# One stage of a hybrid encoder layer: channel sums by two fp32r products, finer pieces of the projections, and KT behind the weights' remainders

## The chip, the cores and the metric

One core of a Trainium2 chip runs the whole layer. The metric is the device time of one execution in microseconds. The kernel before took 826.56 us (median of 3 runs, 826.28 to 828.94).

The engines are named as in the profile: PE (matrix products; PEld is its loading of weights), DVE (vector), ACT (scalar, activations), POOL (GpSimd), SP (issues most DMAs).

## The reference, cut to what matters

One layer over 528 tokens (16 learned ones and 512 of the sequence) of width 1024. A projection of the normalised input feeds two branches of eight heads each, a delta-rule recurrence (RWKV-7) and attention with forgetting (FoX), and a gate for each channel and branch:

```python
u = rmsnorm(h, norm_mix);  proj = u @ w_in
# recurrence: per head and token
kk = k * k_k;  kk = kk / max(sqrt(sum(kk * kk, over the head's 64 channels)), 1e-12)
S = S * w + (S @ -kk) * (kk * a) + v * k;   y = S @ r
bonus = sum(r * k * r_k, over the head's 64 channels) * v
# attention: per head
q = q * rsqrt(mean(q * q, over the head's 64 channels) + eps) * q_gain;  k likewise
# both branches joined, then a squared-ReLU MLP
merged = sig(g_A) * (y_rw @ w_out_rw) + sig(g_B) * (y_fx @ w_out_fx)
h = h + merged @ w_o;  h = h + square(relu(rmsnorm(h) @ w_up)) @ w_down
```

The sums over a head's 64 channels in it (for `kk`, for the bonus, for q and for k) are what the change computes in another way.

## The kernel before, in words

Channels lie on the 128 partitions (two heads in each block of 128 channels, a "pair"), tokens along the free dimension. Most large products take their fp32 operands as two fp32r tensors, an upper part `hi` and a remainder `lo = x - hi`, and add three products (`passes`): hi by hi, hi by lo, lo by hi. ACT makes `whi` and DVE the remainder `wlo` of each piece of weights (`convert`, L548 and L549).

The program has three stages. The first makes the normalised input and the first two projections. The second, from about 30 to 401 us, is the one that the change edits. The third multiplies the two branches' outputs with their output weights (`po`, L1260), and then runs `w_o` and the MLP.

In the second stage several streams are written as generators: the recurrence of four pairs (`recurrent`: `decay`, `keys`, `rows`, `scores`, `bonus` for a pair, `inverse` for a group of two pairs), the sequential part of a group (`chain`) with its `group_norm`, the attention (`attention`), its normalised queries and keys (`fox_features`, `Fox.normed`), and the projections (`projections`), which hold 24 blocks of 128 output columns for the two branches and 16 for the gates. A block takes 24 products for a part of its tokens: branch blocks mostly in two parts of 264 tokens, gate blocks and queries in one of 512.

A stream yields where PE would have to wait, with a function that tells when its data are there by the planner's own clock (`Clock`, with a cost for each engine and the rings of buffers). `Turns.run` takes at each step the first stream by rank whose data are ready: the chain has rank 0, the recurrence 1, attention 2, the features 3, group norm and the splitting of y 4, the projections 8. So the products of the projections fill whatever the others leave, and the last of them are the gate blocks, which nobody needs before the third stage. PE's order in this stage is the planner's order (a manual schedule), and PE takes its instructions in that order: where one has to wait, all behind it wait. The other engines' order is set by priorities in the tile framework.

A projection stream yields before every second `k` in blocks of 264 columns, that is after six products, and before each `k`, after three, in blocks of 512 (L571 and L572 hold the condition and the yield).

The channel sums are products with `ones_blk`, a matrix of two 64x64 blocks of ones, in plain fp32: `pkk` (L906) of the squares of the recurrence's keys, two parts of 264 tokens a pair; `pssq` (L680) of the attention's queries (512 tokens) and keys (two parts of 264); `pbn` (L940) of the bonus, 512 tokens, with `ones_blk` scaled by `r_k` (`rkb`, L934).

`BK` and `KT` are the scaled keys of a pair; `scores` multiplies `BK` with the rows `L` (`psr`, L957) and transposes `KT` (`pbt`, L964). `KT` has one buffer, as have `lc` and `tha`.

The end of the stage: the chain's last step ends in `py` (L1136, L1087); ACT copies it to `y_rw`; `group_norm` (mean, variance, an inverse square root by Newton steps, all on DVE but one square) makes `ysq`; PE transposes it (`pyt`, L1161) and makes the output gate (`pg`, L1164); DVE multiplies, and `divided` splits the result into `ys`, which `po` reads.

## Time and profile before

| | |
|---|---|
| median of 3 runs | 826.56 us |
| the profiled execution | 826.42 us |
| its span, first to last instruction | 824.6 us |
| mean granted clock of PE | 0.998 |
| PE busy in the span | 808.5 us (98%) |
| DVE, ACT, POOL busy | 606.5, 452.7, 120.6 us |
| last projection product to the first of the third stage | about 401 us |

Matmuls are pipelined: the duration of one is longer than the distance to the next, so costs on PE are read from the distance of starts. A line such as L579 is that of a helper or loop for all blocks; tiles tell them apart. The waits that end on PE count; those of other engines count only where PE comes to wait for them.

### The profile page before, as it was taken

Reading aid. Unit: us, or ns where it says so; the run is one execution under the profiler, and the core shown is the slowest. Engines: PE = TensorE matmul, PEld = TensorE weight load, DVE = VectorE, ACT = ScalarE, POOL = GpSimd, SP = SyncE. Lnnn points to the kernel's source line nnn. Section 1 sums busy time; section 2 is a strip of 40 time slices with the busy share of each in tenths; the row PEclk is TensorE's granted clock in tenths of the full one; section 3 lists DMA queues with packets and bytes.
Section 4 is the critical chain, followed back from the end, with each engine's and each line's share of the span. In section 5 each row is a group of like instructions: output and inputs, shape, how many; then the busy total and the mean of one; then the engine's idle time right before and its main releaser. Section 6 shows DMA issues by size and latency. Waiting matters only on the chain.

```text
span 824.6 us, 15506 instructions
## 1 busy us (share of the span) xinstructions
PE 808.5 (98%) x5886; PEld 667.4 (81%) x5886; DVE 606.5 (74%) x1196; ACT 452.7 (55%) x941; POOL 120.6 (15%) x124
## 2 busy tenths in 40 slices
PE   8989999998999999999999999999999999999998
PEld 6979887876987787678888889888888888888886
DVE  6787985687879855875366655875698679867988
ACT  7757538756575457754456534664445434543452
POOL 1021100010011000000032003100740074017300
PEclk9999999999999999999999999999999999999999
DMA  7222221211211412223687405523642365337532
GB/s 232 82 71 71 77 92 48 87 40 65 79 52 52 129 41 66 77 78 116 224 287 227 156 0 154 176 80 113 219 149 82 115 208 159 81 115 228 146 99 76
DMA packets 51483, 95.88 MB, mean 116 GB/s; under 512 B 5832, under 2 KB 7240, under 8 KB 51408
## 3 DMA queue, kind: packets, MB, share of 16 engines
q1 hardware_dynamic: 47680, 86.37, 33.2%
q0 software_dynamic: 1280, 4.20, 1.7%
q10 hardware_dynamic: 2448, 4.33, 1.5%
q8 instruction: 46, 0.75, 0.4%
q14 instruction: 29, 0.24, 0.1%
HBM read 88.56 MB, written 6.31 MB: 115 GB/s over the span
## 4 chain that ended last, share of the span: by engine, by line
PE 86%; DVE 5%; ACT 5%; issue 2%; DMA 1%; SPq 0%; POOL 0%; DVEq 0%; ACTq 0%
PE pj L579 22%; PE po L1350 21%; PE po L1477 12%; PE po L1260 5%; PE pd L1477 5%; PE po L1322 3%; PE pj L394 1%; PE po L1291 1%; PE pd L1291 1%; PE psc L748 1%; PE py L802 1%; PE psr L957 1%; PE ppt L785 1%; PE pch L1108 1%; DVE wlo L549 1%
## 5 line engine op out<-in xcount | busy, mean ns | idle before, releaser
L579 PE MATMUL pj<-uhi,whi 128*128 128x264 f32 (+1 forms) x480 | 164.2, 342 | 0.0
L579 PE MATMUL pj<-uhi,wlo 128*128 128x264 f32 (+1 forms) x480 | 153.8, 320 | 2.5 <-DVE wlo L549 2.5
L579 PE MATMUL pj<-ulo,whi 128*128 128x264 f32 (+1 forms) x480 | 153.8, 320 | 0.0
L242 DVE TENSOR_TENSOR wlo<-wraw,whi 128x512 fp32r<-128x512 f32 x84 | 80.3, 966 | 35.5 <-ACT whi L242 35.5
L579 PEld LDWEIGHTS pj<-uhi,whi 128*128 128x128 f32 x480 | 90.7, 189 | 12.8 <-issue 4.4
L579 PEld LDWEIGHTS pj<-uhi,wlo 128*128 128x128 f32 x480 | 90.7, 189 | 9.5 <-DVE wlo L549 2.9
L579 PEld LDWEIGHTS pj<-ulo,whi 128*128 128x128 f32 x480 | 90.9, 189 | 6.7 <-issue 1.6
L1350 PE MATMUL po<-zlo,whi 128*128 128x512 f32 (+1 forms) x248 | 94.8, 382 | 0.0
L1350 PE MATMUL po<-zhi,wlo 128*128 128x512 f32 (+1 forms) x248 | 94.8, 382 | 0.0
L1350 PE MATMUL po<-zhi,whi 128*128 128x512 f32 (+1 forms) x248 | 94.8, 382 | 0.0
L242 ACT CAST whi<-wraw 128x512 fp32r<-128x512 f32 x84 | 51.4, 617 | 55.7 <-PE po L1350 25.6
L548 ACT CAST whi<-wraw 128x512 fp32r<-128x512 f32 x78 | 47.8, 617 | 42.3 <-PE pj L579 41.6
L549 DVE TENSOR_TENSOR wlo<-wraw,whi 128x512 fp32r<-128x512 f32 x78 | 52.7, 685 | 23.7 <-ACT whi L548 23.0
L276 ACT CAST whi<-t 128x512 fp32r<-128x512 f32 x64 | 39.9, 623 | 44.5 <-DVE wlo L276 27.3
L1477 PE MATMUL po<-wlo,fhi 128*128 128x512 f32 (+1 forms) x164 | 63.4, 387 | 0.1
L1399 POOL TENSOR_TENSOR t<-traw 128x512 f32<-128x512 f32 x24 | 38.2, 1608 | 171.6 <-DMA traw<-in_wdn 171.6
L1477 PE MATMUL po<-whi,flo 128*128 128x512 f32 (+1 forms) x164 | 62.9, 384 | 0.0
L1477 PE MATMUL po<-whi,fhi 128*128 128x512 f32 (+1 forms) x164 | 62.3, 384 | 0.0
L276 DVE TENSOR_TENSOR wlo<-t,whi 128x512 fp32r<-128x512 f32 x64 | 43.6, 690 | 24.2 <-ACT whi L276 24.0
L1366 ACT CAST fhi<-R 128x768 fp32r<-128x768 f32 (+1 forms) x32 | 30.2, 944 | 45.2 <-DVE R L1373 25.3
L1350 PEld LDWEIGHTS po<-zhi,wlo 128*128 128x128 f32 x248 | 46.6, 188 | 9.1
L1350 PEld LDWEIGHTS po<-zhi,whi 128*128 128x128 f32 x248 | 46.6, 188 | 9.0
(330 smaller groups left out, 1708.6 us busy)
## 6 DMA issues: line engine op xcount, KB each, us to landing
wraw<-in_win SPq DMA_DIRECT2D x84, 256.0 KB, 2.7
wraw<-in_wup SPq DMA_DIRECT2D x60, 256.0 KB, 3.1
wraw<-in_wdn SPq DMA_DIRECT2D x48, 256.0 KB, 2.7
traw<-in_wdn SPq DMA_DIRECT2D x48, 256.0 KB, 3.5
gd<-gt ACTq DMA_DIRECT2D x16, 256.0 KB, 2.2
wraw<-in_wout SPq DMA_DIRECT2D x16, 256.0 KB, 3.5
gl<-gd SPq DMA_DIRECT2D x16, 256.0 KB, 3.0
traw<-in_wdn POOLq DMA_DIRECT2D x16, 256.0 KB, 3.2
```

What stands on the lines that cost most here:

```text
L242: casts.append((A.copy(hi, raw), low.tensor_tensor(lo, raw, hi.bitcast(F32), ALU.subtract)))
L276: return A.copy(hi, x), V.tensor_tensor(lo, x, hi.bitcast(F32), ALU.subtract)
L548: after(A.copy(hi, raw), last["ACT"])
L549: after(V.tensor_tensor(lo, raw, hi.bitcast(F32), ALU.subtract), last["DVE"])
L579: mm(po, a, b[:, k, a0:a1], start=n == 0, stop=n == 23)
L1260: mm(po, a, ys[k][:, b, :], start=n == 0, stop=n == 11)
L1291: mm(pd[i], a[:, k, 128 * i:128 * i + 128], b, start=k == 0 and n == 0, stop=k == 7 and n == 2)
L1322: mm(po, a[:, k, 128 * i:128 * i + 128], b[:, k, :], start=n == 0, stop=n == 23)
L1350: mm(po[:, t0:t1], a, b[:, k, t0:t1], start=n == 0, stop=n == 23)
L1366: A.copy(fhi[:, j, a:b], R[:, a:b])
L1399: eng.tensor_tensor(t, sums[c, pair] if c in (T1, T2) else c, d, ALU.add)
L1477: mm(x[i][:, cols], a[:, k, left, 128 * rows:128 * rows + 128], c[:, cols], start=start and k == 0 and n == 0, stop=stop and k == n_pairs ...
```

## The change

Each channel sum becomes two fp32r products with `ones_r` (`summed`): the squares are split into `hi` (a copy on ACT) and `lo` (a subtraction on POOL; for the bonus, on DVE). For the bonus, `r_k` moves from the matrix into the split, and `rkb` is gone. The split parts need room: they take the buffers of `KT`, or for the attention those of `lc` and `tha`, and `held` with `hold` says who has them; the streams `decay`, `keys`, `bonus`, `inverse` and `normed` wait for them. `KT`'s last multiplication and half of `L` stand, for the first pair, behind the last remainder `wlo` issued by then. The transposes of `KT` are planned 1.0 us later than its product. Projection blocks of 264 columns yield after every three products, those of 512 also inside a triple. For pairs after the first, the attention's values are asked for after the queries are normalised.

In the program built from it PE gets 24 more instructions in this stage (48 for 24), POOL 20, ACT 16; DVE has four two-operand ones in place of four scalings, and one copy. The DMAs are the same.

```diff
--- before.py
+++ after.py
+    ones_r = cp.tile([128, 128], F32R, name="ones_r")
...
+    def summed(po, hi, lo):
+        mm(po, ones_r, hi, start=True, stop=False)
+        mm(po, ones_r, lo, start=False, stop=True)
...
+        V.tensor_copy(ones_r, ones_blk)
...
+        low = [None]
...
-                after(V.tensor_tensor(lo, raw, hi.bitcast(F32), ALU.subtract), last["DVE"])
+                low[0] = V.tensor_tensor(lo, raw, hi.bitcast(F32), ALU.subtract)
+                after(low[0], last["DVE"])
...
                         for k in range(KB):
-                            if k % 2 == 0 or a1 - a0 > 300:
+                            if True:
                                 yield lambda f=po is None: max(ck.ready(*w[k // 4]), block_bank()[0] if f else 0.0)
...
                             for a, b in passes(wk(w, k), U):
                                 mm(po, a, b[:, k, a0:a1], start=n == 0, stop=n == 23)
                                 n += 1
+                                if n % 3 == 2 and a1 - a0 > 300:
+                                    yield lambda: 0.0
...
+        held = [0, 0]
+
+        def hold(i):
+            yield lambda: math.inf if held[i] else 0.0
+            held[i] = 1
...
             def normed(self, d, parts, gcol):
                 yield d["in"]
                 f, sq = d["f"], d["sq"]
-                yield lambda: max(ck.ready(sq), banks(len(parts)))
+                c0 = parts[0][0]
+                yield lambda: math.inf if all(held) else 0.0
+                at = held[0]
+                held[at] = 1
+                if at:
+                    hl = rp.tile([128, 2, T], F32R, name="fhl", tag="KT")
+                    hi, lo = hl[:, 0, :], hl[:, 1, :]
+                else:
+                    hi, lo = (rp.tile([128, T], F32R, name="f" + tag, tag=tag) for tag in ("lc", "tha"))
+                d["s"] = A.copy(hi[:, c0:], sq[:, c0:])
+                for a0, a1 in parts:
+                    G.tensor_tensor(lo[:, a0:a1], sq[:, a0:a1], hi[:, a0:a1].bitcast(F32), ALU.subtract)
+                yield lambda: max(ck.ready(lo), banks(len(parts)))
                 pin = None
                 for a0, a1 in parts:
                     pq = psm("pssq")[:, :a1 - a0]
-                    mm(pq, ones_blk, sq[:, a0:a1], start=True, stop=True)
+                    summed(pq, hi[:, a0:a1], lo[:, a0:a1])
...
+                held[at] = 0
...
+                q = yield from x.normed(x.dq, SEQ, qg8)
+                x.q_done.done = True
                 if p > 0:
                     x.ask_values()
-                q = yield from x.normed(x.dq, SEQ, qg8)
-                x.q_done.done = True
...
             def decay(self):
                 p = self.p
+                yield from hold(0)
...
             def keys(self):
 
                 p = self.p
+                yield from hold(1)
...
+                hl = rp.tile([128, 2, T], F32R, name="hl", tag="KT")
+                hi, lo = hl[:, 0, :], hl[:, 1, :]
+                s_ = A.copy(hi, sq[:, :T])
+                for hc in parts:
+                    G.tensor_tensor(lo[:, hc], sq[:, hc], hi[:, hc].bitcast(F32), ALU.subtract)
+                yield lambda: max(ck.ready(hl), banks(2))
+                for hc in parts:
                     pq = psm("pkk")[:, :HT]
-                    mm(pq, ones_blk, sq[:, hc], start=True, stop=True)
+                    summed(pq, hi[:, hc], lo[:, hc])
...
-                V.tensor_tensor(KT, BK, self.P[:, :, 63:64].unsqueeze(2).to_broadcast([128, NCH, 2, 64]), ALU.mult)
+                s_ = V.tensor_tensor(KT, BK, self.P[:, :, 63:64].unsqueeze(2).to_broadcast([128, NCH, 2, 64]), ALU.mult)
+                if p == 0:
+                    after(s_, low[0])
+
+                held[0] = 0
...
-                V.tensor_tensor(l0[:, :, 64:128], r3, P, ALU.mult)
+                s_ = V.tensor_tensor(l0[:, :, 64:128], r3, P, ALU.mult)
+                if self.p == 0:
+                    after(s_, low[0])
...
-                self.rkb = rp.tile([128, 128], F32, name="rkb")
-                after(V.tensor_scalar(self.rkb, ones_blk, self.col(C_RK), None, ALU.mult), last["DVE"])
...
             def bonus(self):
+                yield from hold(1)
+                hl = rp.tile([128, 2, T], F32R, name="hl", tag="KT")
+                hi, lo = hl[:, 0, :S], hl[:, 1, :S]
+                A.activation(hi, self.sq[:, :S], AF.Copy, scale=self.col(C_RK))
+                V.scalar_tensor_tensor(lo, self.sq[:, :S], self.col(C_RK), hi.bitcast(F32), ALU.mult, ALU.subtract)
+                yield lambda: max(ck.ready(hl), banks(1))
                 bp = psm("pbn")
-                mm(bp, rkb, self.sq[:, :S], start=True, stop=True)
+                summed(bp, hi, lo)
+                held[1] = 0
...
             def scores(self):
-                    yield lambda: max(ck.ready(KT), banks(1))
+                    yield lambda: max(ck.ready(KT) + 1.0, banks(1))
...
+                held[1] = 0
...
         def inverse(g, Bms, late):
+            yield from hold(1)
...
+            held[1] = 0
```

Line numbers in the rows below are those of each kernel (after the change `pj` is L588, `po` L1309).

**PE at the end of the second stage.** `pyt` and `pg` are the group norm's transposes and the gate product, `pj` a projection, `ppt` and `ppm` transposes of the attention's weights, `psc` its scores. Before, from the last group norm on:

```order
L1161 MATMUL pyt<-cs,ysq 128x128 x4
L1164 MATMUL pg<-lhi,lw_4209 128x256
L1164 MATMUL pg<-llo,lw_4209 128x256
L1164 MATMUL pg<-lhi,lw_4210 128x256
L1164 MATMUL pg<-lhi,lw_4213 128x256
L1164 MATMUL pg<-llo,lw_4213 128x256
L1164 MATMUL pg<-lhi,lw_4214 128x256
L579 MATMUL pj<-uhi,whi 128x512
L579 MATMUL pj<-ulo,whi 128x512
L579 MATMUL pj<-uhi,wlo 128x512
```

and the last rows ahead of the third stage:

```order
L579 MATMUL pj<-uhi,whi 128x512
L579 MATMUL pj<-ulo,whi 128x512
L579 MATMUL pj<-uhi,wlo 128x512
L1260 MATMUL po<-ys,whi 128x512 x2
L1260 MATMUL po<-ys,wlo 128x512
L1260 MATMUL po<-ys,whi 128x512 x2
```

With the change, from the last gate products on, first to the group norm:

```order
L777 MATMUL psc<-ka,qa 128x272 x2
L777 MATMUL psc<-ka,qa 128x256 x2
L588 MATMUL pj<-uhi,wlo 128x512
L588 MATMUL pj<-uhi,whi 128x512
L588 MATMUL pj<-ulo,whi 128x512
L588 MATMUL pj<-uhi,wlo 128x512
L812 MATMUL ppt<-cs,pm_452 48x128
L814 MATMUL ppt<-cs,pe_5166 128x128 x3
L814 MATMUL ppt<-cs,pe_5174 128x128 x3
L1210 MATMUL pyt<-cs,ysq 128x128 x4
L1213 MATMUL pg<-lhi,lw_4509 128x256
L1213 MATMUL pg<-llo,lw_4509 128x256
```

and from its last gate product on:

```order
L1213 MATMUL pg<-lhi,lw_4514 128x256
L812 MATMUL ppm<-cs,pm_453 48x128
L814 MATMUL ppt<-cs,pe_5360 128x128 x4
L814 MATMUL ppt<-cs,pe_5369 128x128 x4
L828 MATMUL py<-pTm,vm 64x512 x2
L831 MATMUL py<-pT_4920,vt 64x512
L1309 MATMUL po<-ys,whi 128x512 x2
L831 MATMUL py<-pT_4921,vt 64x512
L831 MATMUL py<-pT_4920,vt 64x384
```

Before, 69 gate products stand ahead of the last `pyt` and 57 between `pg` and `po`; with the change the last six stand around `psc`, and after them come `ppt`, `pyt`, `pg`, the attention's last products and `po`, with no projection among them.

**DVE under the same end.** `st`, `rsgy` and `rsgw` are the group norm's, `psc`, `pe` and `pT` the attention's softmax. Before, from the mean to the variance:

```order
L1146 TENSOR_REDUCE st_5133<-y_rw 128x8
L1171 SCALAR_TENSOR_TENSOR yT<-yT,pr,bv 128x256
L276 TENSOR_TENSOR ys<-y_rw,ys 128x512
L1172 TENSOR_TENSOR y_rw<-yT,pg 128x256
L1147 TENSOR_SCALAR st_5133<-st_5133 128x8
L1148 TENSOR_TENSOR y_rw<-y_rw,st_5133 128x2x256
L276 TENSOR_TENSOR ys<-py,ys 128x512
L276 TENSOR_TENSOR ys<-y_fx,ys 128x512
L1152 TENSOR_REDUCE st_5139<-ysq 128x8
L1153 TENSOR_SCALAR st_5139<-st_5139 128x8
```

With the change, in the same place:

```order
L788 ISA pe_5360,nm<-psc,nF_4923 128x272
L788 ISA nm 128x1
L1197 TENSOR_TENSOR y_rw<-y_rw,st_5327 128x2x256
L786 TENSOR_TENSOR psc<-psc,cs 128x128
L788 ISA pe_5369,nm<-psc,nF_4925 128x272
L788 ISA nm 128x1
L788 ISA pe_5360,nm<-psc,nF_4923,nm 128x256
L788 ISA nm 128x1
L1201 TENSOR_REDUCE st_5333<-ysq 128x8
L786 TENSOR_TENSOR psc<-psc,cs 128x128
L1202 TENSOR_SCALAR st_5333<-st_5333 128x8
L817 COPY pT_4920<-ppt 128x3x128
```

The attention's reductions over the last queries now stand between the group norm's instructions; before, there were splits of y.

**DVE around the first pair's KT.** `wlo` is a remainder of weights, `orr` and `ov` are projections' results. Before:

```order
L919 SCALAR_TENSOR_TENSOR BK<-tha,KT 128x9x64
L310 SCALAR_TENSOR_TENSOR orr<-pj,pr_65,tm 128x264
L921 TENSOR_TENSOR KT<-BK,P 128x1152
L930 TENSOR_TENSOR L_662<-orr,P 128x9x64
L549 TENSOR_TENSOR wlo<-wraw,whi 128x512 x2
L306 MEMSET tm 128x1
L549 TENSOR_TENSOR wlo<-wraw,whi 128x512
```

With the change:

```order
L557 TENSOR_TENSOR wlo<-wraw,whi 128x512
L971 TENSOR_TENSOR L_670<-orr,P 128x9x64
L950 SCALAR_TENSOR_TENSOR okk<-okk,pr,sq 128x528
L311 MEMSET tm 128x1
L968 SCALAR_TENSOR_TENSOR L_670<-okk,P 128x9x63
L969 TENSOR_SCALAR L_670<-okk 128x9
L955 SCALAR_TENSOR_TENSOR KT<-okk,lc 128x9x64
L315 SCALAR_TENSOR_TENSOR ov<-pj,pr_66,tm 128x264
L956 SCALAR_TENSOR_TENSOR BK<-tha,KT 128x9x64
L557 TENSOR_TENSOR wlo<-wraw,whi 128x512
L958 TENSOR_TENSOR KT<-BK,P 128x1152
L315 SCALAR_TENSOR_TENSOR ov<-pj,pr_66,tm 128x264
```

KT's product (`KT<-BK,P`) and the half of L from `orr` stood ahead of two remainders; now each stands right behind one.

More of the change, by code (lines that the diff above doesn't have):

```diff
@@ L902, in keys @@
                 s_ = act(sq[:, :T], okr, AF.Square, scale=self.col(C_KK))
-                yield lambda: max(ck.ready(sq), banks(2))
-                for hc in (slice(0, HT), slice(HT, T)):
+                parts = (slice(0, HT), slice(HT, T))
+                hl = rp.tile([128, 2, T], F32R, name="hl", tag="KT")
[5 more added lines that the diff above has]
+                for hc in parts:
                     pq = psm("pkk")[:, :HT]
-                    mm(pq, ones_blk, sq[:, hc], start=True, stop=True)
+                    summed(pq, hi[:, hc], lo[:, hc])
                     V.tensor_scalar(sq[:, hc], pq, 1e-24, None, ALU.max)
```

3 lines of the change are left out of this document (removed).

## The prediction

> **What bounds the kernel now.** I read the page first, then the busy time by stretches, the waits of PE, the chain that ended last, and then the timeline of single engines where the change touches them. The page, with the span and the busy row:
>
> ```profile
> span 824.6 us, 15506 instructions
> PE 808.5 (98%) x5886; PEld 667.4 (81%) x5886; DVE 606.5 (74%) x1196; ACT 452.7 (55%) x941; POOL 120.6 (15%) x124
> ```
>
> By stretches (columns: microseconds, then busy time and count of PE, PEld, DVE, ACT, POOL, then the granted clock, the DMA share and GB/s):
>
> ```profile
> 36.00:371.00 335.00, 325.72 (x3575) 265.26 (x3574) 258.36 (x672) 210.82 (x530) 19.27 (x28) 0.99 0.23 71
> 371.00:401.00 30.00, 30.00 (x141) 24.94 (x138) 14.91 (x33) 13.41 (x25) 0.00 (x0) 1.00 0.39 126
> ```
>
> The whole change lies in the stage from 36 to 401 us, in which one planner weaves the recurrence, the attention and the projections (`pj`) into PE's order. PE is idle there for 335.00 - 325.72 = 9.3 us, and not at all from 371 to 401. So two things set the end of the stage: PE's own work, and whether a filler remains for every wait. The chain of waits shows how large the filler was at the end:
>
> ```profile
> 371.14 15.89 PE pj L579 x69
> 387.46 0.72 PE pg L1164 x6
> 388.18 12.92 PE pj L579 x57
> 401.10 43.81 PE po L1260 x192
> ```
>
> After the attention's last product at 371 come 126 products of gate columns, 28.8 us with no wait in them, and under them the last half of the group norm is finished. This is the row I lean on most: the recurrence ends about 30 us before the stage does, and PE alone bounds the end.
>
> **The change, part by part.**
>
> *The sums.* One fp32 product becomes two fp32r products. Price of each, from the timeline of PE:
>
> ```profile
> 38.33 0.28 PE L579 MATMUL pj<-uhi,wlo 128*128 128x264 f32 x1
> 38.45 1.05 PE L906 MATMUL pkk<-sq,cs 128*128 128x264 f32 x4
> 39.46 0.28 PE L579 MATMUL pj<-ulo,whi 128*128 128x264 f32 x1
> 39.58 0.28 PE L579 MATMUL pj<-uhi,wlo 128*128 128x264 f32 x1
> 65.39 1.02 PE L940 MATMUL pbn<-sq,rkb 128*128 128x512 f32 x2
> 66.25 1.02 PE L680 MATMUL pssq<-fsq,cs 128*128 128x512 f32 x2
> ```
>
> Starts count, not durations. An fp32r product of 264 columns takes 0.12 us (39.46 to 39.58). From 38.45 to 39.46 lie two fp32 sums and one such product, so a sum takes 0.445 us; after the change 0.24, a saving of 0.20. A sum of 512 columns takes 0.86 us (65.39 to 66.25); two fp32r products of 512 take 2 x 0.227 = 0.454 (43.81 us for 192 in the chain above), a saving of 0.41. The counts (the records show two for each sum):
>
> ```profile
> L680 PE MATMUL pssq<-fsq,cs 128*128 128x264 f32 (+1 forms) x24 | 8.4, 459 | 0.0
> L906 PE MATMUL pkk<-sq,cs 128*128 128x264 f32 x16 | 4.2, 386 | 0.0
> L940 PE MATMUL pbn<-sq,rkb 128*128 128x512 f32 x8 | 4.1, 593 | 0.0
> ```
>
> That is 8 + 8 sums of 264 columns and 4 + 4 of 512: 16 x 0.20 + 8 x 0.41 = **6.5 us less PE work**. Bounds: none of it if PE waits instead, 6.5 if all is streamed.
>
> *Finer pieces.* PE pays for each change of form:
>
> ```profile
> 152.77 0.28 PE L579 MATMUL pj<-uhi,wlo 128*128 128x264 f32 x1
> 152.98 0.45 PE L1130 MATMUL pch<-y_fx,bkT 128*64 128x64 f32 x8
> 153.60 0.39 PE L579 MATMUL pj<-uhi,whi 128*128 128x264 f32 x1
> 153.82 0.28 PE L579 MATMUL pj<-ulo,whi 128*128 128x264 f32 x1
> ```
>
> Leaving `pj` costs 0.21 - 0.12 = 0.09, coming back 0.22 - 0.12 = 0.10. In PE's order the `pj` products stand in 94 pieces before and 127 after; counting every neighbour's form, the changes of form in the stage go from 233 to 253, since the new sums have the form of `pj` itself. 20 x 0.1 = **2 us more**; bounds 0 and 33 x 0.2 = 6.6.
>
> *The waits in the middle.* The part on KT and the finer pieces touch these two, the longest of PE's waits:
>
> ```profile
> PE pj L579 <- DVE wlo L549: 2.5, 1, 2.5
> PE pbt L964 <- DVE KT L921: 2.1, 2, 1.3
> ```
>
> ```profile
> 48.09 1.35 DVE L921 TENSOR_TENSOR KT<-BK,P 128x1152 f32<-128x1152 f32 x1
> 49.36 1.82 DVE L930 TENSOR_TENSOR L<-orr,P 128x576 f32<-128x576 f32 x1
> ```
>
> In the first pair KT and half of L, 3.1 us of DVE, ran ahead of the remainders that PE's next block needed. Now a remainder stands ahead of each. What is late next is KT itself: PE reaches KT's transposes one row of scores and one gate product after the scores may start, while DVE still has a remainder and KT's 1.35 us to do, so some tenths of the 2.5 us come back. The other pairs still have KT on their path, but only planned a microsecond later: of 2.1 us I take off 1.5. Together **3.5 us less**; bounds 0 (the wait only moves) and 9.3 (all idle time goes).
>
> *New work on ACT and POOL.* Sixteen copies on ACT and 20 subtractions on POOL. PE does not wait long for them: in PE's order 5 us or more of other products stand between the block that feeds a sum and the sum. But POOL's subtraction reads two operands from SBUF, and this is what such a thing does to DVE here:
>
> ```profile
> 43.92 1.80 POOL L920 TENSOR_TENSOR BK<-sg,lc 128x576 f32<-128x576 f32 x1 [8.01 <-ACT lc L893]
> 44.35 1.40 DVE L928 TENSOR_SCALAR L<-okk 128x9 f32<-128x9 f32 x1
> L928 DVE TENSOR_SCALAR L<-okk x4: 164/717/1399, 44.4 to 248.9; 128x9 f32<-128x9 f32 x4
> ```
>
> Nine elements a partition take 0.16 us alone and 1.40 us when POOL is at work: DVE stands until POOL is through. No row has a POOL subtraction of 264 columns; between nothing and the 1.80 us of the 576-column one, I take 0.8 in proportion, and 1.6 for the four of 512 columns: 16 x 0.8 + 4 x 1.6 = 19 us. If half of that falls on a DVE instruction, DVE loses some 10 us in the stage, in which it is 258 of 335 us busy. Little of that reaches PE: I take **1 us more**, bounds 0 and 10. [...]
>
> *The end of the stage.* Here the order decides. The holds put off pairs and sums, every put-off moment was filled with gate products, and nothing of the 126 remains: after the last six gate products come scores, transposes, the group norm's transposes, and the next stage. So the work that was covered is now waited for. Its length, from the timeline of PE and DVE before:
>
> ```profile
> 367.38 0.45 PE L1087 MATMUL py<-y_fx,Bm 64*64 64x64 f32 x8
> 368.70 0.68 DVE L1146 TENSOR_REDUCE st<-y_rw 128x8 f32<-128x512 f32 x1
> 377.17 0.69 DVE L1156 TENSOR_TENSOR ysq<-y_rw,rsgy 128x512 f32<-128x512 f32 x1
> 386.87 0.60 PE L1161 MATMUL pyt<-cs,ysq 128*128 128x128 f32 x4
> 392.54 0.69 DVE L276 TENSOR_TENSOR ys<-y_rw,ys 128x512 fp32r<-128x512 f32 x1 [0.24 <-ACT ys L276]
> ```
>
> From the last product of the recurrence to the normalised rows: 377.86 - 367.38 = 10.5 us. DVE did 3.7 us of other work in it; after the change it does the attention's softmax of the last 128 queries in the same stretch (estimated from the first two rows below: four reductions, two copies, and scalings and masks like them, some 4 us, against about 2 that leave), so 12 us. (The last two rows, from the chain of waits, are PE's cover, used below.)
>
> ```profile
> 334.43 0.43 DVE L759 CUSTOM_DVE_ANT_0 pe<-psc,nF 128x272 f32<-128x272 f32 x1
> 356.72 1.02 DVE L788 COPY pT<-ppt 128x384 f32<-128x384 f32 x2 [0.25 <-PE ppt L785]
> 348.84 1.09 PE psc L748 x8
> 316.57 0.87 PE ppt L785 x8
> ```
>
> PE has as cover the rest of that product (0.3), six products (6 x 0.227 = 1.4), scores (1.1) and seven transposes (0.8) with changes of form (0.4): 4.0. It stands 8 us; at least 10.5 - 4.0 = 6.5. From there to the split y 393.23 - 386.87 = 6.4 us pass, and PE has about 7 us (transposes, the attention's last products, which took from 367.8 to 371.1, six output products): covered, but the attention's products need copies that now queue on DVE between the group norm's: 0.3 to 2, I take 1. Last, the clock, and the wait that came before it:
>
> ```profile
> 202.85 1.23 PE L748 MATMUL psc<-ka,qa 64*128 64x256 f32 x4 [1.52 <-DVE nm L759]
> 203.00:205.00 2.00, 2.00 (x18) 1.31 (x20) 1.65 (x6) 0.27 (x1) 0.00 (x0) 0.71 0.00 0
> 205.00:207.00 2.00, 2.00 (x16) 1.88 (x13) 2.00 (x7) 1.57 (x4) 0.28 (x2) 0.50 0.00 0
> ```
>
> After a wait of 1.5 us the granted clock fell to half for over 3 us, which cost 2 x 0.29 + 2 x 0.50 = 1.6 us. Eight idle microseconds should do so too; part of the slow work lies under DVE, so 1 us. [...] The end of the stage costs **10 us**, bounds 6.5 and 13.
>
> *Sum.* -6.5 + 2 - 3.5 + 1 + 10 = +3.0. The profiled execution took 826.42 us (span 824.6 and 1.8 around it), so 829.4; the median of the runs shown is 0.14 above it: **829.5 us**.
>
> **Rivals.** About 2.5 us (0.3%) is what a measurement of this kernel can tell from no change.
>
> *Faster: the middle gives back more than the end takes.* The pieces of three products let a ready stream in sooner, and the waits of the middle go nearly all. For: the idle 9.3 us consists of waits of at most 2.5 us. Against: the rows name DVE as releaser, and DVE gets more work. If 8 of 9.3 us go and the end costs 7.5: -6.5 + 2 - 8 + 7.5 + 0.5 = -4.5, so **822**. It decides from where the middle's idle time falls below about 3.5 us.
>
> *No change:* as forecast, but the end costs 7 (no clock drop, shorter softmax): **826.5**.
>
> *Clearly slower: POOL holds DVE on the recurrence's path.* If a third of the 20 subtractions each stop a copy on which PE waits for 0.9 us, 6 us more instead of 1: **834.5**. For it the L928 row, against it that DVE has 77 us free.
>
> *KT's part only moves its wait* from the products to the transposes: 2 us of the 3.5 don't come, **831.5**, inside the forecast.
>
> **How the numbers follow.** The forecast, with the KT rival, has 0.36 and its own range 827 to 834; the POOL rival 0.13; no change 0.25; faster 0.26. Slower by over 0.3% takes most of the first two: 0.46; within 0.3%: 0.28; faster: 0.26. The sum of the low bounds is far out (-6.5 + 0 - 9.3 + 0 + 6.5 = -9.3, 817), and so is that of the high ones; the range from 820 to 836 reaches to both rivals' prices and a little beyond.
>
> **What would show it.** Right: between the last gate product and the first long run of `po` PE stands some 8 us ahead of `pyt` for DVE, and the clock row there shows less than 1.00; two-product sums in 0.24 and 0.45 us; less idle time in the middle by some 3 us; short DVE instructions stretched beside POOL's subtractions. Wrong: a `pyt` that is not waited for, gate products left at the end, or middle idle time grown above 9 us.

## The result, and the profile after

The changed kernel took **837.37 us** (median of 4 runs, 833.61 to 841.55) beside 827.34 us for the kernel before on the same chip: a ratio of 1.0112, 95% interval 1.0084 to 1.0140. It is slower, as the likeliest case said, but by 10 us and not by 3, and it lies above the range that ended at 836. A second set of four runs on another occasion gave 834.73 us (ratio 1.0085, 1.0058 to 1.0112). All eight runs lie between 833.0 and 841.6; the runs of the kernel before lie mostly within 3 us of each other. The two sets' profiles are of the longest and of the shortest of the eight, so the other six lie between them.

The first profile is that of 841.55 us (span 839.8). Its page:

```profile
span 839.8 us, 15549 instructions
PE 815.9 (97%) x5886; PEld 671.9 (80%) x5886; DVE 607.2 (72%) x1197; ACT 461.1 (55%) x957; POOL 138.4 (16%) x144
```

The third stage is as long as before: the long run of `po` starts at 416.81 us (401.10 before), so 423.0 us are left, beside 423.5. The whole loss is in the second stage. By stretches (the columns are those of the table shown of before):

```profile
36.00:392.00 356.00, 345.84 (x3637) 284.97 (x3635) 260.02 (x660) 224.09 (x548) 38.08 (x49) 0.99 0.25 77
392.00:399.00 7.00, 5.10 (x39) 2.98 (x37) 5.85 (x19) 4.50 (x9) 0.00 (x0) 0.99 0.22 75
399.00:404.00 5.00, 0.22 (x1) 0.25 (x2) 4.43 (x21) 1.60 (x5) 0.00 (x0) 0.50 0.14 52
404.00:417.00 13.00, 13.00 (x42) 7.03 (x42) 4.03 (x8) 3.55 (x10) 0.00 (x0) 0.54 0.25 82
```

Up to 392 us PE is idle for 10.2 us; before it was 9.3 in all. From 392 to 404 another 6.7 us are idle, and the last 13 us run at a granted clock of 0.54. The longest waits of PE:

```profile
PE pyt L1210 <- DVE ysq L1205: 5.9, 1, 5.9
PE py L1185 <- ACT y_rw L1137: 2.4, 1, 2.4
PE pw L1077 <- issue: 1.8, 1, 1.8
...
PE pbt L1010 <- DVE KT L958: 0.6, 1, 0.6
```

The wait of 2.5 us for `wlo` in the first pair is gone, and of 2.1 us for KT 0.6 are left. In their place stand two waits that the kernel before did not have at this length, for `y_rw` and inside the inverse's products of L1077, and the one that was forecast, ahead of `pyt`. The end of the stage on PE and DVE:

```profile
392.61 0.45 PE L1136 MATMUL py<-y_fx,Bm 64*64 64x64 f32 x8
...
397.38 0.55 PE L814 MATMUL ppt<-cs,pe 128*128 128x128 f32 x3 [0.54 <-DVE nm L788]
...
402.94 0.69 DVE L1205 TENSOR_TENSOR ysq<-y_rw,rsgy 128x512 f32<-128x512 f32 x1
403.78 1.09 PE L1210 MATMUL pyt<-cs,ysq 128*128 128x128 f32 x4 [5.85 <-DVE ysq L1205]
...
416.74 0.50 PE L1309 MATMUL po<-ys,wlo 128*128 128x512 f32 x1
```

The recurrence ends at 393 us, with six gate products behind its last `py`; before it ended at 368, with 126 behind it. And the sums do what was worked out: four products of 264 columns, 0.12 us apart, are two sums in 0.24 us each.

```profile
198.85 0.28 PE L280 MATMUL pkk<-hl,ones_r 128*128 128x264 f32 x1
198.97 0.28 PE L281 MATMUL pkk<-hl,ones_r 128*128 128x264 f32 x1
199.09 0.28 PE L280 MATMUL pkk<-hl,ones_r 128*128 128x264 f32 x1
199.21 0.28 PE L281 MATMUL pkk<-hl,ones_r 128*128 128x264 f32 x1
```

### The profile page after: what moved, and what is told of

Its sections match the earlier page's. It is cut to its first block, busy times and chain, and to the rows that moved or that the text cites. A ratio compares the mean times of both kernels' runs of the same rounds, so it can differ in the third digit from the quotient of the medians.

```text
span 839.8 us, 15549 instructions
## 1 busy us (share of the span) xinstructions
PE 815.9 (97%) x5886; PEld 671.9 (80%) x5886; DVE 607.2 (72%) x1197; ACT 461.1 (55%) x957; POOL 138.4 (16%) x144
## 4 chain that ended last, share of the span: by engine, by line
PE 79%; DVE 10%; ACT 7%; issue 3%; DMA 1%; SPq 1%; POOL 0%; DVEq 0%; ACTq 0%
PE po L1399 21%; PE pj L588 17%; PE po L1526 12%; PE po L1309 5%; PE pd L1526 5%; PE po L1371 3%; PE py L831 1%; PE pj L399 1%; PE pd L1340 1%; PE po L1340 1%; DVE wlo L557 1%; PE psc L777 1%; DVE pe L788 1%; PE psr L1003 1%; PE pch L1157 1%
## 5 line engine op out<-in xcount | busy, mean ns | idle before, releaser
L588 PE MATMUL pj<-uhi,whi 128*128 128x264 f32 (+1 forms) x480 | 161.5, 336 | 0.3 <-ACT qa L674 0.3
L588 PE MATMUL pj<-uhi,wlo 128*128 128x264 f32 (+1 forms) x480 | 158.3, 330 | 0.0
L588 PE MATMUL pj<-ulo,whi 128*128 128x264 f32 (+1 forms) x480 | 154.9, 323 | 0.0
L243 DVE TENSOR_TENSOR wlo<-wraw,whi 128x512 fp32r<-128x512 f32 x84 | 81.1, 977 | 30.6 <-ACT whi L243 30.6
L588 PEld LDWEIGHTS pj<-uhi,whi 128*128 128x128 f32 x480 | 91.7, 191 | 11.5 <-issue 3.6
L588 PEld LDWEIGHTS pj<-uhi,wlo 128*128 128x128 f32 x480 | 91.7, 191 | 8.1 <-issue 2.0
L588 PEld LDWEIGHTS pj<-ulo,whi 128*128 128x128 f32 x480 | 91.9, 191 | 5.8
L557 DVE TENSOR_TENSOR wlo<-wraw,whi 128x512 fp32r<-128x512 f32 x78 | 54.5, 709 | 30.5 <-ACT whi L556 30.2
```

Source lines behind the costliest of these rows:

```text
L243: casts.append((A.copy(hi, raw), low.tensor_tensor(lo, raw, hi.bitcast(F32), ALU.subtract)))
L557: low[0] = V.tensor_tensor(lo, raw, hi.bitcast(F32), ALU.subtract)
L588: mm(po, a, b[:, k, a0:a1], start=n == 0, stop=n == 23)
```

## The experiments

Ratios are to the kernel before on the same chip and occasion (827.8 to 828.5 us in the medians). "Left behind" counts the gate products that PE's order has behind a stream's last `pch` (recurrence) or last scores `psc` (attention): they are the cover of the stage's end. The kernel before has 129 and 168, the changed one 25 and 4.

### The changed kernel again

> The changed kernel once more, for a second profile. Its first one took 841.55 us, with 16.8 us of idle PE in the stage and three stretches at half clock (after waits of 1.8, 2.4 and 5.9 us). Theory A (the recurrence ends late, no gate products are left to cover its tail): the wait of some 6 us ahead of pyt stands again, 833 to 842 us. If the two waits in the middle (1.8 us inside the products of L1077 with no releaser, 2.4 us for y_rw) belong to the order of the work, both stand again too; if they are chance, the profile is some 5 to 8 us shorter and they are gone.

834.73 us, and the profiled execution is one of 833.01 us. The waits of 5.9 and 2.4 us stand again, that of L1077 is 1.0 us instead of 1.8: all three belong to the order. What differs is the clock. In this profile the middle runs at full clock, and the end is at half for 6.8 us instead of 17.1 (2.1 and 4.9 of these pass inside the wait itself):

```profile
393.00:399.00 6.00, 0.31 (x2) 0.34 (x3) 5.34 (x24) 2.10 (x7) 0.00 (x0) 0.80 0.18 69
399.00:404.00 5.00, 5.00 (x23) 3.83 (x21) 2.75 (x6) 2.61 (x7) 0.00 (x0) 0.55 0.02 3
404.00:408.00 4.00, 4.00 (x20) 1.85 (x18) 1.29 (x3) 0.79 (x2) 0.00 (x0) 1.00 0.69 223
```

From `pyt` to the long run of `po` it needs 408.13 - 398.69 = 9.4 us, the first profile 416.74 - 403.78 = 13.0, with the same products.

### Each part alone

Theory A: the sums put the recurrence off, no gate products are left, and the tail of the group norm is waited for. Theory B: POOL's subtractions hold DVE. Theory C: the pieces cost it.

```diff
 attention_only: before, with in Fox.normed
+    (holds, hi = A.copy(sq), lo on POOL)    summed(pq, hi, lo)
     q = normed(...);  x.ask_values()        # as in the change: asked behind q's norm
 recurrence_only: before, with in keys and bonus
+    hl in KT's place, no holds              summed(pq, hi, lo);  summed(bp, hi, lo)
 fine_only: before, with in projections
-    if k % 2 == 0 or a1 - a0 > 300:
+    if True:
+    if n % 3 == 2 and a1 - a0 > 300: yield lambda: 0.0
```

> The kernel before with two-product sums in the attention's norms alone (8 sums of 264 columns, 4 of 512), with the holds they need; the recurrence keeps fp32 sums, the pieces stay as before, and KT is where it was. Saved: 8 x 0.20 + 4 x 0.41 = 3.2 us. In its order 126 gate products stand behind the recurrence, as before. Theory A: PE alone bounds the end, so about 3 us faster, 824 beside 827.3 (0.996). Theory B (POOL's subtractions hold DVE): 12 of the 20 subtractions are here, so 60% of that loss, 827 to 833. Theory C (the loss comes from pieces and their changes of form): 824, as A.

841.31 us, ratio 1.0157 (1.0131 to 1.0182): slower by 13 us where every theory had it within 5. Theory A failed in its form: the recurrence's last `pch` stands at 370 us, 6 us later than before and still covered, and yet the stage ends at 416. This time the attention is late. The sums of its third queries stand at 270 us (195 before), of its fourth at 343 (292 before), and the last scores come when no product is left to fill. PE then waits 2.3 us for the softmax. Most of the loss is clock: PE is idle for 3.9 us more than before, and runs at half clock for 27 us of the stage, before for 3.4.

> The kernel before with two-product sums in the recurrence alone (8 of 264 columns, 4 of 512), each in the place of KT, with no holds since one stream uses that place in turn; the attention keeps fp32 sums. Saved: 3.2 us of PE. In its order the first inverse stands some 10 us later than before and 75 gate products (17 us) are left behind the recurrence, against 126 before and 25 after the change. Theory A: the recurrence is late by 8 to 10 us, but what is left still covers its tail, so about 3 us faster, 824 to 826. Were the holds without effect, it would lose like the changed kernel, 830 or more. Theory B: 8 of 20 subtractions, 826 to 831.

834.87 us, 1.0078 (1.0053 to 1.0104). PE waits 2.6 us for the subtraction on POOL of a key's square (`PE pkk <- POOL hl`), and the profile has two stretches at half clock, of 3.4 us each at 85 and 215 us. 75 products left behind were not enough to bring the 3.2 us out. Theories A and B had it lower; what came is what was expected of holds without effect, 830 or more: this run has none and loses like the changed kernel.

> The kernel before with the finer pieces alone (264-column blocks let others in after every 3 products, 512-column blocks inside their threes); sums, slots and KT as before. In its order the changes of form go from 233 to 257, and the gate products left behind the recurrence from 126 to 145. Theory A: the recurrence is not late, so only the changes cost: 24 x 0.1 = 2.4 us, less what of the middle's 9.3 us of waiting goes; 826 to 829.5. Theory C: pieces cost about 5 us and more, 832.

829.51 us, 1.0017 (1.0006 to 1.0028): 1.4 us slower (0.5 to 2.3). The pieces alone cost somewhat less than the 2.4 us that their changes of form were priced at. Theory C falls.

### What makes the attention late

The change moves one call that the prediction did not price: the request for a pair's value block (`ask_values`) goes behind the norm of q.

```diff
 ask_later: before, in fox_features
-                if p > 0:
-                    x.ask_values()
                 q = yield from x.normed(x.dq, SEQ, qg8)
                 x.q_done.done = True
+                if p > 0:
+                    x.ask_values()
 attention_asked_early: attention_only with the same lines put back
```

> The kernel before with one line moved: the attention asks for a pair's value block only behind the norm of q, as the changed kernel does. No new sums, no holds, no new pieces. Theory D (this request is what makes the attention late: its third norm stood at 194 us before and at 268 us in the run with the attention's sums alone, its fourth at 291 and 341): the attention's last scores stand behind the last gate product, their softmax is waited for with little to cover it, 834 to 841 us. Theory E (holds and the longer way of a split sum make the streams late, the request does not matter): 826 to 829.

836.46 us, 1.0098 (1.0075 to 1.0121): that line alone costs 8 us, with fp32 sums, no holds and the old pieces. Not all of it is lost at the end: of the profile's 11 us, idle PE and half clock behind the last gate product have some 6, and three stretches at half clock in the middle (13.7 us together, 3.4 before) most of the rest. The chain of waits ends in the attention, with no gate product behind it:

```profile
389.01 5.95 PE pj L579 x26
398.22 0.73 ACT pe L762 x2
404.97 1.71 PE ppt L785 x8
406.67 1.90 PE py L799 x4
408.57 3.63 PE py L802 x16
412.20 43.75 PE po L1260 x192
```

> The run with the attention's sums alone (841.3 us), with the request for the value block back ahead of q's norm; two-product sums, copies, subtractions on POOL and holds stay. In its order 84 gate products are left behind the recurrence and 99 behind the attention's last scores (0 without this edit). Theory D: the 13 us go, and the saving of 3.2 us shows, 824 to 828. Theory E: the holds and the split stay, so it stays slow, 835 to 841.

831.70 us, 1.0043 (1.0026 to 1.0060). Ten of the 13 us go, against theory E; theory D had all of them go and the saving show, in a range that ended 4 us lower. The end is now covered (42 gate products behind the attention); the waits of the middle stand (3.0 us for `wlo` at 49 us), and half clock behind two of them (6.8 us from 51.8 us on, 3.4 from 212).

### The clock at the end

```diff
 filled_wait: after, in group_norm, ahead of the transposes pyt
+            if g and c0:
+                for i in range(22):
+                    mm(pos.rearrange("p a b -> p (a b)"), uhi[:, 0, :128], uhi[:, 1, :512], start=True, stop=True)
```

> The changed kernel with 22 products of 512 columns, whose result is overwritten, ahead of the last four transposes pyt, where PE waits 5.9 us for the group norm: 22 x 0.227 = 5.0 us of work inside the wait. Theory F (the granted clock falls to half because PE stands idle there, and stays low for some of the stage's last products and the first of the next stage): no half clock at the end of the stage, 831 to 833 us, and runs closer together than the 833 to 842 of the changed kernel. If the clock has nothing to do with the wait: 835 to 838 as without them.

830.97 us, 1.0033 (1.0020 to 1.0046), five runs within 0.9 us, where the changed kernel spread over 8. The timeline of its end:

```profile
392.80 5.28 PE L1211 MATMUL pg<-uhi 128*128 128x512 f32 x22
398.81 0.63 PE L1213 MATMUL pyt<-cs,ysq 128*128 128x128 f32 x4 [0.73 <-DVE ysq L1205]
403.15 2.38 PE L831 MATMUL py<-pT,vt 128*64 128x512 f32 x16
405.46 0.74 PE L1312 MATMUL po<-ys,whi 128*128 128x512 f32 x2
```

The same wait, filled with products that nobody reads, costs 4 to 6 us less: from `pyt` to `po` 6.65 us, or 7.1 with the two `po` that the changed kernel does earlier, instead of 9.4 and 13.0. Theory F holds: 2.3 and 5.9 us of the end were the clock. The two profiles say the same from the other side: behind the wait PE ran 4.8 and 12.2 us at half clock, counted by half 2.4 and 6.1 us of lost work (the products `pj` of 264 columns start 0.22 us apart at half clock, at 196 us of the first profile, and 0.12 apart at full). The row of the end is the firm one here. The whole times also differ by the middle, which is at full clock in this run's profile and was not in the first; why all five runs were free of such stretches (granted clock 0.998 and more), the products at the end cannot say.

### Which edits bring the saving out

The next versions change two things: where the request stands, and which engine subtracts.

```diff
 sums_only_mended: after, without the finer pieces and KT's part, with
+   x.ask_values() ahead of q's norm
-   G.tensor_tensor(lo[:, hc], sq[:, hc], ...)      # keys, on POOL
+   V.tensor_tensor(lo[:, hc], sq[:, hc], ...)      # on DVE
 mended: after, with these two edits alone (finer pieces and KT's part stay)
 no_bonus_sum: sums_only_mended, the bonus in fp32, all subtractions on DVE
 no_finer_pieces: after, with the pieces of before
 subtract_on_DVE: after, with all 20 subtractions on DVE
```

> All two-product sums of the change, without its finer pieces and its part on KT; the request for the value block stays ahead of q's norm, and the recurrence's subtractions run on DVE, the attention's on POOL. Saved: 6.5 us of PE and some changes of form. In its order 57 gate products are left behind the recurrence and 96 behind the attention's last scores. Theory D with the late subtraction as second cause (PE waited 2.6 us for it where the recurrence's sums were alone): 820 to 823 us. Theory E: 829 to 835, since the holds are all there.

833.12 us, 1.0060 (1.0034 to 1.0085): far above theory D's range, and inside theory E's. The end is covered, but PE reached the first inverse 7.0 us before DVE had finished `AX` for it, and half clock came with it (6.8 us from 120.6 us on, and 3.4 us at 134.9). The holds alone do not bring this: the next run has them all.

> The changed kernel with two edits: the request for the value block back ahead of q's norm, and the recurrence's subtractions on DVE instead of POOL. Sums, finer pieces, holds and KT's part stay. In its order 64 gate products are left behind the recurrence and 114 behind the attention's last scores (25 and 4 in the changed kernel). Theory D (late streams leave the end uncovered, and its waits bring half clock): the 5.9 us wait ahead of pyt and the half clock of the end go, so 826 to 830. If the pieces and the split itself cost the time, 833 to 837 as the changed kernel.

**824.46 us, 0.9950 (0.9934 to 0.9966): faster than the kernel before.** Its stage, with the end of its chain of waits:

```profile
36.00:397.00 361.00, 351.57 (x3708) 287.40 (x3705) 273.50 (x708) 232.41 (x566) 32.65 (x40) 1.00 0.25 77
```

```profile
382.36 13.61 PE pj L588 x60
396.40 0.70 PE pg L1213 x6
397.11 43.63 PE po L1309 x192
```

PE is idle for 9.4 us, as before; no wait is longer than 1.4 us, the granted clock is 1.00 throughout, and 60 gate products stand ahead of the last `pyt`. The stage ends 4.0 us earlier than before: 1.7 of these are the half clock that the profile of before has at 204 us and this one has not, and 2.3 are less work on PE.

> The changed kernel with the coarser pieces of before; all else stays. In its order the changes of form go from 256 to 238, but no gate product is left behind the recurrence (25 with the finer pieces). Theory G (the pieces cost PE 0.15 us for each change of form, and help no stream): 18 x 0.15 = 2.7 us faster than the changed kernel, 831 to 834. Theory D: the recurrence is later still and the end less covered, so what the changes give is lost there, 834 to 839.

835.63 us, 1.0092 (1.0077 to 1.0107). The wait ahead of `pyt` is 8.8 us, as theory D has it for a recurrence without products behind it. Theory G, which had it faster than the changed kernel, falls.

> The changed kernel with all 20 subtractions on DVE instead of POOL; nothing else is edited. In its order 75 gate products are left behind the recurrence (25 with POOL), but none behind the attention's last scores, since the request for the value block stays late. Theory B (POOL holds DVE; its subtractions took 0.75 to 1.9 us, with DVE instructions beside them stretched from 0.48 to 1.66): faster by 5 us and more, 829 to 831. Theory D: the recurrence is earlier, but the attention's end stays uncovered, 832 to 838.

846.48 us, 1.0217 (1.0200 to 1.0234), the slowest of all and outside both expectations. The recurrence is covered, the attention is not (the sums of its fourth queries stand at 347 us), DVE is fuller, and four stretches run at half clock (6.8, 3.4, 3.4 and 13.6 us). The 1.66 us in the expectation, from a profile of the changed kernel, stands beside POOL's product for `BK` (L957, 259.26 us, 1.82 us long), not beside a subtraction. It speaks against theory B, though not cleanly, since the order moves with it.

> All two-product sums but the bonus's, all subtractions on DVE, the request ahead of q's norm, pieces and KT as before. Saved: 16 x 0.20 + 4 x 0.41 = 4.8 us of PE. In its order 93 gate products are left behind the recurrence and 135 behind the attention's last scores, the most of all versions with sums. Theory D: the end is covered, and what is left of the saving after the shorter waits of the middle shows: 822 to 827. If holds and splits themselves cost what the sums save, wherever the end stands: 829 to 833.

835.89 us, 1.0092 (1.0075 to 1.0108), a miss for theory D: here both ends are covered, and the loss is in the middle. PE waits 2.0 us for DVE at 118 us and 1.8 us inside the second inverse at 302, half clock of 6.8 us comes with each, and a third stretch as long stands at 211, where no wait is longer than 0.4 us. The windows of the first:

```profile
118.00:122.00 4.00, 1.31 (x129) 1.19 (x128) 3.74 (x7) 1.06 (x2) 0.00 (x0) 1.00 0.30 84
122.00:129.00 7.00, 6.90 (x198) 6.59 (x199) 2.08 (x5) 0.19 (x1) 0.00 (x0) 0.51 0.19 69
```

So a covered end is needed, but a stage with longer waits in its middle can lose as much.

### One edit at a time, and what the other parts are worth

```diff
 asked_early: after, with the request ahead of q's norm (first edit of mended)
 recurrence_on_DVE: after, with the keys' subtractions on DVE (second edit)
 mended_coarse: mended, with the pieces of before
 mended_without_KT: mended, without
-                if p == 0: after(s_, low[0])
-   ck.ready(KT) + 1.0
```

> The changed kernel with one edit: the request for the value block ahead of q's norm. POOL still subtracts. In its order 93 gate products stand behind the attention's last scores (4 before this edit), but 1 behind the recurrence (25). Theory D, with both ends needed: the group norm's wait ahead of pyt stays or grows, 6 to 9 us, and with it the half clock, 832 to 837 us. If the attention's end alone were to blame: 824 to 827.

839.09 us, 1.0127 (1.0097 to 1.0156), 2 us above theory D's range and 12 above the other.

> The changed kernel with one edit: the recurrence's eight subtractions on DVE, the attention's stay on POOL, the request stays late. In its order 72 gate products are left behind the recurrence (25), none behind the attention's last scores. Theory D, with both ends needed: the wait for the group norm goes, that for the last softmax stays, 832 to 840. If POOL's hold on DVE in the recurrence were to blame: 824 to 828.

838.29 us, 1.0108 (1.0073 to 1.0144). This is within theory D's range. Neither edit alone gains anything; both together gain 10 us and more. The first waits of PE in each of the two runs say why. With the attention early, the recurrence is the stream that ends uncovered:

```profile
PE pyt L1210 <- DVE ysq L1205: 12.8, 2, 9.2
```

With the recurrence early, the attention is:

```profile
PE ppm L812 <- ACT pm L797: 2.9, 1, 2.9
```

The first has some 10 us at half clock at the stage's end, the second some 14.

> The version of 824.5 us with the coarser pieces of before. In its order 9 changes of form fewer, the first inverse 9 us later (84 beside 75 us by the order's own count), and 33 gate products behind the recurrence instead of 64. If the finer pieces only cost changes of form: 823. If they let the recurrence's splits in sooner and so keep the end covered: 829 to 834, with a wait for the group norm or half clock behind a wait in the middle.

827.46 us, 0.9989 (0.9973 to 1.0006). Both expectations missed: the finer pieces are worth 3 us here. Without them PE waits 2.2 us for `y_rw` and 1.5 for `fsq`, and half clock follows both (3.4 us at 175 us, 10.2 at 210); with them no such wait is left. The recurrence's end is covered in both.

> The version of 824.5 us with KT and half of L back ahead of the remainders in the first pair, and no microsecond of planned delay for the transposes of KT. The prediction's term: of the 3.5 us, the wait of PE for wlo at 49 us (2.5 us before) comes back, and the transposes of KT wait again, 826 to 828. If KT's part only moves its wait: 824 to 825.

824.20 us, 0.9948 (0.9929 to 0.9968): beside the finer pieces KT's part is worth nothing that can be measured, and the 2.5 us wait for `wlo` does not come back. With the pieces of before it is worth some 6 us: sums_only_mended and mended_coarse differ by KT's part alone, 1.0060 beside 0.9989, and the wait of 7.0 us at the first inverse stands only where it is left out. So each of the two parts does what the other would have done, and a part's worth holds only for the version that it is tried in.

## Why the prediction was wrong in size

*What bounds the kernel: right.* Before, PE alone bounds the end of the stage, and 126 products cover it. Where that cover was kept and no long wait arose (824.46 us), part of the saving on PE came out.

*The sums, -6.5: right as a price, and it did not stay.* A sum of 264 columns takes 0.24 us in the rows above, one of 512 is two products of 0.23. PE's busy time in the stage, counted by half where the clock was at half, is 354 us before, 348 in sums_only_mended and 351.5 in the version of 824.46 us. In the changed kernel it is 353 to 354 again: what the sums save, PE spends on something else.

*Finer pieces, +2: right in size* (+1.4, 0.5 to 2.3, alone; by the busy time just named, the changed kernel without them has 1 to 2 us less), and the text did not see that they also shorten waits: in the version of 824.46 us they gain 3 us.

*The waits in the middle, -3.5: wrong, and the first of the two steps that failed.* The two waits that were named did shrink, by 2.5 and 1.5 us, and others of 2.4 and 1.0 to 1.8 us came. Idle time up to 392 us is 10.2 us (9.3 in the second profile up to the same place, 387 us) against 9.3, so the prediction's own sign of being wrong, idle time in the middle above 9 us, came. The rival "KT's part only moves its wait" was right that those microseconds would not come, but not that the transposes of KT would take them: they wait 0.6 us.

*POOL blocking DVE, +1: the blocking was seen, its consequence was not.* Beside one of the new subtractions a DVE instruction stands for 1.24 us; one of the same form takes 0.23 (timeline of the changed kernel):

```profile
108.06 0.23 DVE L1042 TENSOR_TENSOR tmp<-AX,AX 128x78 f32<-128x78 f32 x1
...
300.79 1.29 POOL L704 TENSOR_TENSOR ftha<-fsq,flc 128x512 fp32r<-128x512 f32 x1 [11.89 <-ACT flc L702]
300.93 1.24 DVE L1042 TENSOR_TENSOR tmp<-AX,AX 128x78 f32<-128x78 f32 x1
```

But the recurrence's subtractions mattered in another way: moved to DVE, they leave 72 gate products behind the recurrence instead of 25. The likely reason, not tried by itself, is their own length on the way to its next product. The groups of the changed kernel and of the 824.46 us version (least, median and longest in ns):

```profile
L939 POOL TENSOR_TENSOR hl<-sq,hl x8: 743/850/1882, 39.1 to 265.3; 128x264 fp32r<-128x264 f32 x8
```

```profile
L939 DVE TENSOR_TENSOR hl<-sq,hl x8: 407/423/756, 39.9 to 248.5; 128x264 fp32r<-128x264 f32 x8
```

The prediction counted this work as DVE's loss and "little of that reaches PE". But the planner spends every such delay on gate products, and they are the cover of the end.

*The end of the stage, +10: the mechanism was right, its last term, the clock, was not, and this is the second step that failed.* The stretch of the group norm was forecast at 12 us, it took 403.63 - 392.61 = 11.0; PE stood 6.7 us (0.29, 0.54 and 5.85), forecast 8. "Last, the clock" was put at 1 us. It cost 5.9 us in the first profile and 2.3 in the second, and filling the wait took it away. The step had said that part of the slow work lies under DVE; in the first profile the half clock instead lasted through nearly all of the stage's remaining products. As a whole the term came to 9.0 and 12.6 us, inside its bounds, because the wait was shorter than forecast. And the sum has no clock for the middle, where the first profile lost another 4.7 us.

*The cause that the prediction gave for the lost cover was not the one that decides.* "The holds put off pairs and sums": the version of 824.46 us has every hold and is covered, if by 64 products instead of 129; and recurrence_only, which has none, loses 7 us. What the holds take of the cover was not tried by itself. What decides is the later request for the value block (8 us by itself) together with the recurrence's subtractions on POOL: either alone leaves one stream uncovered, and the cost of a second one does not add.

*The sum again.* In the second profile, 6.6 us longer than the one before: -6.5 for the sums, +6.7 idle (15.9 against 9.3), +2.3 for the clock at the end, less 1.6 that the clock cost before: 0.9. In the first, 15.1 us longer: -6.5, +7.5 idle, +5.9 clock at the end, and in the middle 10.2 us at half clock (the windows below, of the first profile), with PE at work in 9.4 of them, which is 4.7 us of lost work less the same 1.6: 10.0. In both 5 to 6 us are left over, where the prediction had 3 for pieces and POOL. They are not idle time but PE's own busy time, as the paragraph on the sums shows; 1 to 2 are the pieces, the rest stays open. So of the step from the forecast 3.0 to the 6.6 us of the second profile, the waits that did not go are 3.5 and this rest 2.7, while the end (1.0) and the clock of before (1.6) came out better than forecast.

```profile
137.00:143.00 6.00, 6.00 (x111) 5.70 (x111) 1.80 (x4) 0.64 (x2) 0.00 (x0) 0.51 0.01 3
...
194.00:198.00 4.00, 4.00 (x22) 4.00 (x21) 3.00 (x9) 3.13 (x11) 0.00 (x0) 0.57 0.02 4
```

As to its rivals: POOL holding DVE came nearest in time (834.5) and by another mechanism than it named; "no change" and "faster" had the middle giving back what the end takes, and the middle gave nothing back.

## What to carry to other kernels

Where one engine is nearly always busy and filler work covers the end of a stage, ask for every stream, not only for the longest, what still stands behind its last product: here a change that delays two streams was mended only by mending both. A wait of the matrix engine has to be priced with the clock that was lost behind such waits (here 2.3 and 5.9 us, in two profiles, behind the same wait of 5.9), and a range has to hold that it changes from run to run; filling the wait with dead products is a quick way to measure it. A moved request for data is part of the change, however small the line.

## What the runs showed of the hardware that was not expected

The same wait in the same place does not always cost clock. Up to 52 us the run with the later request does what the kernel before does, and PE has the same wait of 2.5 us for `wlo` at 49 us. The windows of before:

```profile
46.00:52.00 6.00, 3.53 (x28) 3.10 (x27) 6.00 (x9) 3.40 (x8) 2.86 (x5) 1.00 0.06 14
52.00:58.00 6.00, 6.00 (x70) 4.46 (x71) 5.35 (x13) 2.75 (x7) 0.00 (x0) 1.00 0.55 175
```

and of the run with the later request:

```profile
46.00:52.00 6.00, 3.54 (x27) 3.05 (x26) 6.00 (x9) 3.40 (x8) 2.86 (x5) 1.00 0.06 14
52.00:56.00 4.00, 4.00 (x35) 2.81 (x33) 2.69 (x8) 0.67 (x2) 0.00 (x0) 0.60 0.73 221
```

At full clock in the one, at half for 3.4 us in the other. The wait of 2.4 us for `y_rw` brought 3.4 us at half clock in one profile of the changed kernel and none in the other, that of 5.9 us brought 17.1 and 6.8. In all the profiles that have half clock inside the stage, its stretches took 3.4, 6.8, 10.2, 13.6 or 17.1 us, that is one to five times 3.41. In the first profile of the changed kernel they began at 136.1, 194.1 and 398.9 us, 58.0 and 204.8 us apart, which is 17 and 60 times 3.41. Half clock came with waits of 1.5 us (the kernel before, from 203.8 us on) and 3.0 us (attention_asked_early, from 51.8); what decides whether a wait brings half clock, no run shows. What the clock took in the stage was 2 to 11 us in the two profiles of the changed kernel, as much as the change itself.

Half clock also came without a long wait. In the run with the later request it comes at 288.3 us, and in the seven microseconds before PE waits 0.31 us at most; about 3.3 of them it spends on the inverse's products of 32x32:

```profile
281.00:288.30 7.30, 6.99 (x275) 5.83 (x277) 4.23 (x7) 2.28 (x5) 0.00 (x0) 1.00 0.59 182
288.30:295.20 6.90, 6.90 (x96) 2.81 (x91) 1.41 (x2) 0.00 (x0) 0.00 (x0) 0.51 0.01 2
```

The version without KT's part has the same for 3.4 us at 121.3 us, behind waits of 0.5 and 0.3. The kernel before does these products at full clock (1.00 from 280 to 300 us), so that they are the cause is not shown.

What stays open is the wait of 0.9 to 2.2 us inside the inverse's products (L1077), which the profile gives no releaser for; it stands in most versions with new sums in the recurrence, and 0.3 us of it in the fastest. In the changed kernel it is 1.0 us where the clock stays full and 1.8 where half clock begins while it lasts, so its length there may be the clock's doing rather than the clock's cause.
